# Turning operands with one vector instruction and sixteen on-chip transfers in a two-layer transformer trunk

## The chip, the cores and the metric

One NeuronCore of one Trainium2 chip runs the kernel. The metric is the device time of one execution in microseconds (us). TensorE is called PE here, VectorE DVE, ScalarE ACT, GpSimd POOL, and SP is the engine whose queue issues nearly all DMAs of this kernel.

## What is computed

Two layers of a transformer trunk on 256 tokens of width 2048, in float32. Cut to the lines that matter here:

```python
for i in range(2):
    if i == 0: h = h + even_mixer(h)   # sparse attention and gated linear attention
    else:      h = h + odd_mixer(h)    # q, k, v = split(rmsnorm(h) @ w_in); 16 heads, z = q @ k.T ...
    xn = rmsnorm(h, ffn_norm[i])
    h = h + (silu(xn @ w_gate) * (xn @ w_up)) @ w_down        # hidden width 5632
    gate = sigmoid(rmsnorm(h, ple_norm[i]) @ ple_w_gate[i])
    h = h + (p[i] @ ple_w_proj[i]) * gate
out = rmsnorm(h, final_norm)
```

PE sums over the partitions. So the left operand of each product, which has tokens along the partitions when it is made, has to be turned until its columns lie along the partitions.

## The kernel before, in words

**The stream of weights.** Every product with a weight matrix goes through `unit` (line 176): four chunks of 128 rows by 512 columns, 1 MB, come by one DMA on SP's queue (line 184) into a tile `raw`, of which there are two. For each half of it ACT casts a rounded part `whi` (line 99) and DVE subtracts it from `raw` for the rest `wlo` (line 100); there are four of each. PE then runs 12 products of 512 columns for a half, 24 for a unit (lines 201 to 203): left high part by `whi`, left high part by `wlo`, left low part by `whi`, for each chunk and each of the two halves of the tokens. A `block` (line 206) is the row of units, mostly four, that makes 512 output columns.

**Order of the work.** `later` (line 161) puts small pieces of work into a line, and `tick` (line 169) runs at most one of them after each half unit. A scheduler then orders the instructions of each engine, and each engine takes its own in that order. An instruction that waits holds up what stands behind it on its engine. That goes for SP too: a DMA whose source is not ready holds up the later ones. The program uses eight completion semaphores in turn for SP's DMAs, so a DMA also waits until the one eight places ahead has landed.

**Where operands are turned.** Three places, two ways:

- `h`, five times, for the norms after the first: `finish_cols` (line 224) takes each 512 columns of `h` when they are final, squares them on ACT, and queues two calls of `turn_h` (line 135). Each call turns two chunks of 128 columns by four PE transposes against an identity (line 141) into PSUM; ACT multiplies by the gain for the high part (line 146), DVE makes the low part (line 147). The first norm does the same while `x` arrives.
- the FFN's hidden block `sl` (line 802): four calls of `turn_blocks` (line 123), each four DVE transposes of 32 partitions by 256 columns (line 128) that write another quarter of the partitions; DVE turns blocks of 32 by 32. Then ACT and DVE split the result `hx` (lines 789, 790). There are 22 such blocks.
- q and k of the odd mixer, two tiles for each of four groups of heads, by `turn_blocks` as well, into `qT` and `kT`, which `scores` reads.

**Around them.** `mixer_out` (line 674) runs the first two output blocks in two parts, so that with 16 units its four column blocks end after units 6, 8, 12 and 16. The last `down` (line 809) of an FFN has two units a block, as 11 hidden blocks go in groups of 3, 3, 3 and 2. `gated` (line 861) is the sigmoid and two DVE operations on each half of the tokens. In the last stage `keep` (line 892) loads a quarter of the last columns' weights into a tile of its own, `kept`, four times.

Of the kernel before, what the change touches and what calls it, by code (L numbers as in the profile page):

```python
# [27 lines left out]
def trunk_kernel(ctx: ExitStack, tc: tile.TileContext, x, p, even_norm, even_w_in, even_w_gk,  # L28
# [36 lines left out]
    # the activation tables and the tensor engine's clock are up when the data comes  # L65
# [7 lines left out]
    # norm gains, one row of 128 per chunk, turned so that a chunk's gains lie along the partitions  # L73
# [61 lines left out]
    def turn_h(dst, norm, c2):  # L135
        """Chunks 2*c2 and 2*c2+1 of h, transposed, times the gain, split."""
# [39 lines left out]
    def unit(ps, stat, k0, cols, first, last, nk=KU, kw0=None, step=KU, pre=None):  # L176
        """nk chunks of the contraction: cols = [(weight, first column, width)]."""
# [28 lines left out]
    def block(stat, cols, nk=KC, key=None, ps=None, k0=0, k1=None, kw=0, pre=None):  # L206
        """Output columns over chunks k0..k1 of the contraction; returns the two PSUM tiles."""
# [43 lines left out]
    with tc.issue_after(got_gains.ins):  # L251
# [4 lines left out]
    # upb[s, c] = 1/16 where s <= c in one chunk of 64; sub[s, c] = 1/16 where s > c there  # L256
    upb = const.tile([P, P], F32, name="upb")
    nc.gpsimd.memset(upb, 0.0625)
    nc.gpsimd.affine_select(upb, upb, pattern=[[1, P]], compare_op=OP.is_ge, fill=0.0, base=0,
                            channel_multiplier=-1)  # L260
    nc.gpsimd.memset(upb[0:64, 64:128], 0.0)
    sub = stage("sub")[:, :P]
    nc.gpsimd.memset(sub, 0.0625)
    nc.gpsimd.affine_select(sub, sub, pattern=[[-1, P]], compare_op=OP.is_gt, fill=0.0, base=0,
                            channel_multiplier=1)
    nc.gpsimd.memset(sub[64:128, 0:64], 0.0)
    subr = const.tile([P, P], F32R, name="subr")
    nc.vector.tensor_copy(subr, sub)
    # keys no later than the query, in one chunk
    upm = upb.bitcast(I32)  # L270
    # strictly earlier keys, keys along the partitions
# [8 lines left out]
    # -1 where the first index is no earlier than the second  # L280
# [10 lines left out]
    def even_mixer(xs, ps0, ep):  # L291
# [3 lines left out]
        oT = new_act()  # L295

# [12 lines left out]
        def tokens(ps, name, w=NB):  # L309
            """The block's last w columns by tokens, scaled by the row's norm."""  # L310
# [7 lines left out]
        # u0: c (128), the last pair of q_idx (128), k_idx (64), zeros (64), k_idx again (64),  # L318
        # the gate's low-rank part (16), one
# [6 lines left out]
        # c and three pairs of q_idx  # L326
# [8 lines left out]
        # a pair of q_idx, k_idx, w_idx and the gate's low-rank part  # L335
# [71 lines left out]
        def index_heads(pairs, tt):  # L407
            """pairs: [(the pair's columns by tokens, its first head)]"""
# [574 lines left out]
```

## Time and profile before

| | |
|---|---|
| Median of 3 runs | 2440.72 us (2440.68 to 2441.49) |
| Profiled execution, first to last instruction (span) | 2438.5 us |
| Time beside the span (median less span) | 2.2 us |
| PE busy | 2417.6 us, 99% |
| DVE busy | 1506.6 us, 62% |
| ACT busy | 1154.1 us, 47% |
| DMA queue of SP | 447 MB, 55.6% of 16 engines' span |
| TensorE clock granted | nine tenths or more of full speed in all 40 slices |

The profile was taken of one execution, whose own time is known by its span alone; the median stands 2.2 us above it. Busy times are unions of instructions on an engine. Products overlap in PE's pipeline, so the mean duration of one is longer than the distance between two.

### The profile page before, as it was taken

To read this page: it belongs to the slowest core of one execution; us is meant where nothing else is said; L and a number is where in the kernel's file an instruction comes from. 1 tells how busy PE (TensorE), PEld (TensorE's weight loads), DVE (VectorE), ACT (ScalarE), POOL (GpSimd) and SP (SyncE) were. 2 spreads that over 40 slices of the span, in tenths; PEclk is the share of its full clock that TensorE was granted. 3 is DMA by queue.
4 is the path that set the end of the run, shared out by engine and by line. 5 is a ranking of instruction groups with operands and counts; after the bars stand their busy time and mean duration, and the time that the engine had idled before them with its cause. 6 is when DMAs were issued, how large, how long until landed. Compare 5 with 4: busy or idle time off the path is not lost.

```text
span 2438.5 us, 27647 instructions
## 1 busy us (share of the span) xinstructions
PE 2417.6 (99%) x10966; PEld 1996.5 (82%) x10966; DVE 1506.6 (62%) x1907; ACT 1154.1 (47%) x1418; POOL 19.2 (1%) x45
## 2 busy tenths in 40 slices
PE   8999999999999999999999999999999999999998
PEld 7887788888888888888888888888888888888887
DVE  5765555766756665655676666557667556556564
ACT  6644444344434434446546565544444344444463
POOL 0000000000000000000000000000000000000000
PEclk9999999999999999999999999999999999999999
DMA  6454455566556565555554454555655655556563
GB/s 211 147 169 151 144 194 186 189 196 201 189 192 193 186 205 183 198 190 185 178 190 156 161 184 165 180 190 177 203 190 192 205 190 186 196 187 206 182 231 123
DMA packets 231651, 450.01 MB, mean 185 GB/s; under 512 B 9457, under 2 KB 16337, under 8 KB 231394
## 3 DMA queue, kind: packets, MB, share of 16 engines
q1 hardware_dynamic: 231234, 447.07, 55.6%
q8 instruction: 86, 1.41, 0.2%
q10 hardware_dynamic: 288, 1.18, 0.1%
q14 instruction: 43, 0.35, 0.0%
HBM read 446.12 MB, written 2.10 MB: 184 GB/s over the span
## 4 chain that ended last, share of the span: by engine, by line
PE 91%; issue 5%; ACT 2%; DVE 1%; DMA 1%; SPq 0%; POOLq 0%; POOL 0%; DVEq 0%; ACTq 0%
PE mm L202 29%; PE mm L201 29%; PE mm L203 29%; PE at L141 1%; DVE kT L128 1%; DVE wlo L100 0%; DMA raw<-in_odd_w_in_dram 0%; PE at L424 0%; DMA h<-in_x_dram 0%; PE at L742 0%; DVE sp L719 0%; ACT whi L99 0%; ACT sp L716 0%; ACT sp L715 0%; ACT L715 0%
## 5 line engine op out<-in xcount | busy, mean ns | idle before, releaser
L100 DVE TENSOR_TENSOR wlo<-raw,whi 128x1024 fp32r<-128x1024 f32 (+2 forms) x848 | 1020.7, 1213 | 794.1 <-ACT whi L99 790.1
L99 ACT CAST whi<-raw 128x1024 fp32r<-128x1024 f32 (+2 forms) x848 | 874.8, 1042 | 1053.5 <-PE mm L203 668.8
L201 PE MATMUL mm<-whi,aH 128*128 128x512 f32 (+2 forms) x2656 | 1036.9, 390 | 0.7 <-ACT whi L99 0.7
L202 PE MATMUL mm<-wlo,aH 128*128 128x512 f32 (+2 forms) x2656 | 1028.8, 387 | 4.1 <-DVE wlo L100 4.1
L203 PE MATMUL mm<-whi,aL 128*128 128x512 f32 (+2 forms) x2656 | 1028.7, 387 | 0.0
L202 PEld LDWEIGHTS mm<-wlo,aH 128*128 128x128 f32 x2656 | 499.4, 188 | 104.7 <-DVE wlo L100 5.9
L203 PEld LDWEIGHTS mm<-whi,aL 128*128 128x128 f32 x2656 | 499.1, 188 | 103.4 <-issue 1.0
L201 PEld LDWEIGHTS mm<-whi,aH 128*128 128x128 f32 x2656 | 499.2, 188 | 102.9 <-issue 2.8
L201 PE MATMUL mm<-whi,hH 128*128 128x512 f32 x704 | 277.2, 394 | 0.0
L202 PE MATMUL mm<-wlo,hH 128*128 128x512 f32 x704 | 277.0, 393 | 0.0
L203 PE MATMUL mm<-whi,hL 128*128 128x512 f32 x704 | 273.6, 389 | 0.0
L128 DVE STREAM_TRANSPOSE hx<-sl 32x256 f32<-32x256 f32 x352 | 153.6, 436 | 6.1
L201 PEld LDWEIGHTS mm<-whi,hH 128*128 128x128 f32 x704 | 132.2, 188 | 30.0
L203 PEld LDWEIGHTS mm<-whi,hL 128*128 128x128 f32 x704 | 132.2, 188 | 29.7
L202 PEld LDWEIGHTS mm<-wlo,hH 128*128 128x128 f32 x704 | 132.4, 188 | 26.1
L146 ACT ACTIVATE aH<-at,gT 128x256 fp32r<-128x256 f32 x96 | 45.1, 473 | 51.4 <-DVE aL L147 47.5
L789 ACT CAST hH<-hx 128x1024 fp32r<-128x1024 f32 x22 | 23.2, 1054 | 92.6 <-DVE hx L128 92.6
L147 DVE SCALAR_TENSOR_TENSOR aL<-at,gT,aH 128x256 fp32r<-128x256 f32 x96 | 45.8, 480 | 22.0 <-ACT aH L146 21.9
L234 DVE TENSOR_TENSOR h<-mm,h 128x512 f32<-128x512 f32 x80 | 52.4, 682 | 2.7 <-PE mm L203 2.7
L141 PE MATMUL at<-ident,h 128*128 128x128 f32 x192 | 30.5, 283 | 5.0 <-DMA h<-in_x_dram 5.0
L141 PEld LDWEIGHTS at<-ident,h 128*128 128x128 f32 x192 | 24.9, 145 | 11.8 <-DMA h<-in_x_dram 3.0
L128 DVE STREAM_TRANSPOSE qT<-tok 32x256 f32<-32x256 f32 x64 | 27.9, 436 | 6.8 <-ACT tok L762 5.8
(221 smaller groups left out, 806.8 us busy)
## 6 DMA issues: line engine op xcount, KB each, us to landing
raw<-in_ffn_w_gate_dram SPq DMA_DIRECT2D x88, 1024.0 KB, 5.2
raw<-in_ffn_w_up_dram SPq DMA_DIRECT2D x88, 1024.0 KB, 5.2
raw<-in_ffn_w_down_dram SPq DMA_DIRECT2D x88, 1024.0 KB, 5.0
raw<-in_odd_w_in_dram SPq DMA_DIRECT2D x48, 1024.0 KB, 5.2
raw<-in_even_w_in_dram SPq DMA_DIRECT2D x36, 1024.0 KB, 5.0
raw<-in_ple_w_gate_dram SPq DMA_DIRECT2D x28, 1024.0 KB, 5.1
raw<-in_even_w_out_dram SPq DMA_DIRECT2D x16, 1024.0 KB, 5.1
raw<-in_odd_w_out_dram SPq DMA_DIRECT2D x16, 1024.0 KB, 5.0
```

What stands on the lines that cost most here:

```text
L99: nc.scalar.copy(hi, raw)
L100: nc.vector.tensor_tensor(lo, raw, hi.bitcast(F32), OP.subtract)
L128: nc.vector.transpose(dst[32 * a:32 * a + 32, :, :, 32 * q:32 * q + 32], src.rearrange("p t (m a c) -> p t m a c", a=4, c=32)[32 * q:32 * ...
L141: nc.tensor.transpose(ps[:, c, tt, :], h[:, tt, k * P:(k + 1) * P], ident)
L146: nc.scalar.activation(dst[0][:, k, :], src, AF.Copy, scale=g)
L147: nc.vector.scalar_tensor_tensor(dst[1][:, k, :], src, g, dst[0][:, k, :].bitcast(F32), op0=OP.mult, op1=OP.subtract)
L201: nc.tensor.matmul(ps[tt][:, :n], sh, hi[:, c, :n], start=st, stop=False)
L202: nc.tensor.matmul(ps[tt][:, :n], sh, lo[:, c, :n], start=False, stop=False)
L203: nc.tensor.matmul(ps[tt][:, :n], sl, hi[:, c, :n], start=False, stop=en)
L234: nc.vector.tensor_tensor(hs, ps[tt], hs, OP.add)
L789: nc.scalar.copy(d[0], t)
```

## The change

All operands after the first norm are turned in two steps. `cross` first runs one DVE transpose on all 128 partitions and 1024 columns: it turns each block of 32 by 32 where it lies, so that within each quarter of the partitions the columns come in the right place but tokens of four quarters stay apart. Then 16 DMAs on SP's queue, 32 KB each, carry 32 partitions of `tq` to 32 partitions of `tx`: each source quarter to each destination quarter. ACT and DVE read `tx` (views `crossed` and `flat` put it in order) and split it. `turn_blocks` goes, and `turn_h` remains for the first norm alone. The pool of `tq` (one buffer) and `tx` (two) is opened after the even mixer. To make room, the squares share the one buffer of the tag `stage`, two constants move into the even mixer's pool, the sigmoid's result stays in PSUM, and `keep` takes its place among the two `raw` tiles.

```diff
-    def turn_blocks(dst, src, a):
-        for q in range(4):
-            nc.vector.transpose(dst[32 * a:32 * a + 32, :, :, 32 * q:32 * q + 32],
-                                src.rearrange("p t (m a c) -> p t m a c", a=4, c=32)[32 * q:32 * q + 32, :, :, a, :])
+    pools = {}
+    def cross(src):
+        tq = pools["x"].tile([P, 4, NT, 4, 32], F32, name="tq", bufs=1)
+        nc.vector.transpose(tq.rearrange("p a t m r -> p t m a r"),
+                            src.rearrange("p t (m a c) -> p t m a c", a=4, c=32))
+        x = pools["x"].tile([P, 8, 4, 32], F32, name="tx")
+        for a in range(4):
+            for q in range(4):
+                nc.sync.dma_start(x[32 * a:32 * a + 32, q::4], tq[32 * q:32 * q + 32, a])
+        return x
+    def crossed(x):
+        return x.rearrange("p q m r -> p m q r")
+    def flat(t):
+        return t.rearrange("p m (q r) -> p m q r", q=8)
...
+    def gain_h(dst, norm, x, c2):
+        for k in (2 * c2, 2 * c2 + 1):
+            g = gT[1][:, (norm - 1) * KC + k:(norm - 1) * KC + k + 1]
+            src = crossed(x)[:, k % 4]
+            hi, lo = (flat(d[:, k:k + 1, :])[:, 0] for d in dst)
+            nc.scalar.activation(hi, src, AF.Copy, scale=g)
+            nc.vector.scalar_tensor_tensor(lo, src, g, hi.bitcast(F32), op0=OP.mult, op1=OP.subtract)
...
     def finish_cols(nx, cb):
         for tt in range(NT):
             square_sum(nx["key"], tt, cb, h[:, tt, cb * NB:(cb + 1) * NB])
+        x = {}
+        first = (nx["key"], "x", cb)
+        later(lambda: x.update(x=cross(h[:, :, cb * NB:(cb + 1) * NB])), key=first)
         for c2 in (2 * cb, 2 * cb + 1):
-            later(lambda c2=c2: turn_h(nx["dst"], nx["norm"], c2), key=(nx["key"], c2))
+            later(lambda c2=c2: gain_h(nx["dst"], nx["norm"], x["x"], c2), key=(nx["key"], c2), after=(first, 2))
...
-                for a in range(4):
-                    later(lambda t=t, d=dst, a=a: turn_blocks(d.rearrange("p t (m c) -> p t m c", c=P), t, a))
+                x = {}
+                later(lambda t=t, x=x: x.update(x=cross(t)), key=("x3", g, i))
+                later(lambda d=dst, x=x: nc.scalar.copy(flat(d), crossed(x["x"])), after=(("x3", g, i), 2))
...
-                hx = fp.tile([P, 4, NT * P], F32, name="hx")
-                for a in range(4):
-                    later(lambda d=hx, t=sl, a=a: turn_blocks(d.rearrange("p m (t c) -> p t m c", t=NT), t, a))
-                later(lambda t=hx, n=n, gi=gi: split_hid(hT[gi], t, 4 * n), key=("hT", i, b))
+                x = {}
+                later(lambda t=sl, x=x: x.update(x=cross(t)), key=("xT", i, b))
+                later(lambda x=x, n=n, gi=gi: split_hid(hT[gi], x["x"], 4 * n), key=("hT", i, b),
+                      after=(("xT", i, b), 2))
...
-            raw = pp.tile([P, KU, HB], F32, name="kept", bufs=1)
+            raw = wp.tile([P, KU, NB], F32, name="raw", bufs=2)[:, :, :HB]
```

**What the order of the instructions becomes.** Three places. In the names, `raw` is a unit's 1 MB of weights, `tq` the tile after the DVE transpose, `tx` the tile after the transfers; the numbers tell buffers of the same name apart.

SP at an FFN block's end, before: the four loads of the next block's weights.

```order
L184 DMA raw_3435<-in_ffn_w_gate_dram 128x4x512
L184 DMA raw_3473<-in_ffn_w_gate_dram 128x4x512
L184 DMA raw_3515<-in_ffn_w_gate_dram 128x4x512
L184 DMA raw_3555<-in_ffn_w_gate_dram 128x4x512
L184 DMA raw_3594<-in_ffn_w_up_dram 128x4x512
```

Now:

```order
L208 DMA raw_3473<-in_ffn_w_gate_dram 128x4x512
L208 DMA raw_3526<-in_ffn_w_gate_dram 128x4x512
L208 DMA raw_3562<-in_ffn_w_gate_dram 128x4x512
L135 DMA tx_3509<-tq_3507 32x2x128 x16
L208 DMA raw_3596<-in_ffn_w_gate_dram 128x4x512
```

The sixteen transfers stand between the third and the fourth load. All 22 FFN blocks and the eight tiles of q and k have this pattern.

SP in the last `down` of the first FFN (its eight units are raw_7794 to raw_8130), now; before, the same loads stood in a row:

```order
L208 DMA raw_7924<-in_ffn_w_down_dram 128x4x512
L208 DMA raw_7970<-in_ffn_w_down_dram 128x4x512
L135 DMA tx_7907<-tq_7905 32x2x128 x16
L208 DMA raw_8027<-in_ffn_w_down_dram 128x4x512
L135 DMA tx_8010<-tq_8008 32x2x128 x16
L208 DMA raw_8073<-in_ffn_w_down_dram 128x4x512
L135 DMA tx_8113<-tq_8111 32x2x128 x16
L208 DMA raw_8130<-in_ffn_w_down_dram 128x4x512
```

Three times sixteen transfers stand among the last three loads, one load between two of them.

DVE at the same place, now: mm_7968 and mm_7969 are the sums of the third column block.

```order
L261 TENSOR_TENSOR h_73<-mm_7968,h_73 128x512
L261 TENSOR_TENSOR h_73<-mm_7969,h_73 128x512
L130 STREAM_TRANSPOSE tq_8111<-h_73 128x8x4x32
L172 SCALAR_TENSOR_TENSOR aL_7791<-tx_8010,gT5_95,aH_7790 128x256 x4
L100 TENSOR_TENSOR wlo_8076<-raw_8073,whi_8075 128x1024
L100 TENSOR_TENSOR wlo_8096<-raw_8073,whi_8095 128x1024
```

The subtraction for the seventh unit (raw_8073) stands behind the sums of the third block, which end when that seventh unit should begin on PE; before, the same subtractions (raw_7998 is the seventh unit there, mm_7902 and mm_7903 are the sums) stood ahead of them, with one for the eighth (raw_8041):

```order
L100 TENSOR_TENSOR wlo_8001<-raw_7998,whi_8000 128x1024
L100 TENSOR_TENSOR wlo_8017<-raw_7998,whi_8016 128x1024
L147 SCALAR_TENSOR_TENSOR aL_7730<-at_7938,gT5_95,aH_7729 128x256 x2
L100 TENSOR_TENSOR wlo_8044<-raw_8041,whi_8043 128x1024
L147 SCALAR_TENSOR_TENSOR aL_7730<-at_7965,gT5_95,aH_7729 128x256
L234 TENSOR_TENSOR h_73<-mm_7902,h_73 128x512
L147 SCALAR_TENSOR_TENSOR aL_7730<-at_7965,gT5_95,aH_7729 128x256
```

The work that waits for PE's last product of the block has moved ahead of the subtractions that PE's next unit needs.

## Rows read from the trace of the kernel before

**Rows 1.** The page, part 1: busy time of each engine.

```profile
PE 2417.6 (99%) x10966; PEld 1996.5 (82%) x10966; DVE 1506.6 (62%) x1907; ACT 1154.1 (47%) x1418; POOL 19.2 (1%) x45
```

**Rows 2.** Waits of PE: who waited for whom, us in total, times, longest.

```profile
PE mm L202 <- DVE wlo L100: 4.1, 5, 0.8
PE mm L201 <- ACT whi L99: 0.7, 2, 0.5
```

**Rows 3.** Timeline of PE round one turn of `h`: start us, us, what.

```profile
1200.20 0.39 PE L202 MATMUL mm<-wlo,aH 128*128 128x512 f32 x1
1200.43 0.39 PE L203 MATMUL mm<-whi,aL 128*128 128x512 f32 x1
1200.66 0.60 PE L141 MATMUL at<-ident,h 128*128 128x128 f32 x4
1201.02 0.48 PE L201 MATMUL mm<-whi,aH 128*128 128x512 f32 x1
1201.33 0.40 PE L202 MATMUL mm<-wlo,aH 128*128 128x512 f32 x1
```

**Rows 4.** Groups by line and shape: count, busy us, mean ns, idle before.

```profile
L141 PE MATMUL at<-ident,h 128*128 128x128 f32 x192 | 30.5, 283 | 5.0 <-DMA h<-in_x_dram 5.0
L128 DVE STREAM_TRANSPOSE hx<-sl 32x256 f32<-32x256 f32 x352 | 153.6, 436 | 6.1
L147 DVE SCALAR_TENSOR_TENSOR aL<-at,gT,aH 128x256 fp32r<-128x256 f32 x96 | 45.8, 480 | 22.0 <-ACT aH L146 21.9
L100 DVE TENSOR_TENSOR wlo<-raw,whi 128x1024 fp32r<-128x1024 f32 x832 | 1010.4, 1223 | 779.8 <-ACT whi L99 775.9
L99 ACT CAST whi<-raw 128x1024 fp32r<-128x1024 f32 x832 | 865.5, 1050 | 1040.2 <-PE mm L203 661.2 <-DMA raw<-in_ffn_w_up_dram 152.9 <-DMA raw<-in_odd_w_in_dram 68.9
```

**Rows 5.** Timeline of SP: three small transfers issued in a row.

```profile
17.39 0.33 SPq L80 DMA_DIRECT2D graw<-in_ffn_norm_dram  x1
17.77 0.42 SPq L80 DMA_DIRECT2D graw<-in_ple_norm_dram  x1
18.23 0.42 SPq L80 DMA_DIRECT2D graw<-in_odd_norm_dram  x1
```

**Rows 6.** DMA issues: count, KB each, median us to landing; then line L80's landings.

```profile
raw<-in_ffn_w_gate_dram SPq DMA_DIRECT2D x88, 1024.0 KB, 5.2
kept<-in_ple_w_gate_dram SPq DMA_DIRECT2D x4, 512.0 KB, 6.0
...
DMA to landing us min/median/max: 1.6/2.8/4.2
```

**Rows 7.** Timelines of SP, ACT and DVE round one end of an up block.

```profile
757.38 0.37 SPq L184 DMA_DIRECT2D raw<-in_ffn_w_gate_dram  x1
766.29 0.37 SPq L184 DMA_DIRECT2D raw<-in_ffn_w_gate_dram  x1
...
760.48 1.05 ACT L99 CAST whi<-raw 128x1024 fp32r<-128x1024 f32 x1 [1.67 <-PE mm L203]
763.20 1.06 ACT L99 CAST whi<-raw 128x1024 fp32r<-128x1024 f32 x1 [1.67 <-PE mm L203]
...
759.99 1.40 DVE L802 SCALAR_TENSOR_TENSOR sl<-mm,rstd,sl 128x512 f32<-128x512 f32 x2
761.43 3.57 DVE L128 STREAM_TRANSPOSE hx<-sl 32x256 f32<-32x256 f32 x8
765.03 1.23 DVE L100 TENSOR_TENSOR wlo<-raw,whi 128x1024 fp32r<-128x1024 f32 x1
```

**Rows 8.** Timelines of ACT and DVE at a gated block's end.

```profile
1147.45 1.27 ACT L864 ACTIVATE sgm<-mm,rstd 128x512 f32<-128x512 f32 x2
...
1149.38 1.28 DVE L867 TENSOR_TENSOR h<-h,sgm 128x512 f32<-128x512 f32 x2
```

**Rows 9.** Windows after the last product: busy times, granted clock, DMA share, GB/s.

```profile
2431.00:2434.00 3.00, 0.00 (x0) 0.00 (x0) 1.59 (x5) 1.15 (x3) 0.56 (x1) 1.00 0.19 72
2434.20:2438.40 4.20, 0.00 (x0) 0.00 (x0) 0.00 (x0) 0.00 (x0) 0.00 (x0) 0.50 0.54 181
```

More of the change, by code (lines that the diff above doesn't have):

```diff
@@ L107, in square_sum @@
             ss[key] = sm.tile([P, NT, 4], F32, name="ss")
-        scr = sm.tile([P, NB], F32, name="sqs", bufs=1)
+        scr = sm.tile([P, NB], F32, name="sqs", tag="stage", bufs=1)
         nc.scalar.activation(scr, src, AF.Square, accum_out=ss[key][:, tt, cb:cb + 1])
@@ L253, in trunk_kernel @@
     done.update((("n0", i), 0) for i in range(KC // 2))
[L257 to L270, printed above, removed]
     diag = const.tile([P, P], F32, name="diag")
@@ L295, in even_mixer @@
         oT = new_act()
+        upb = ep.tile([P, P], F32, name="upb", bufs=1)
+        nc.gpsimd.memset(upb, 0.0625)
+        nc.gpsimd.affine_select(upb, upb, pattern=[[1, P]], compare_op=OP.is_ge, fill=0.0, base=0,
+                                channel_multiplier=-1)
+        nc.gpsimd.memset(upb[0:64, 64:128], 0.0)
+        sub = stage("sub")[:, :P]
+        nc.gpsimd.memset(sub, 0.0625)
+        nc.gpsimd.affine_select(sub, sub, pattern=[[-1, P]], compare_op=OP.is_gt, fill=0.0, base=0,
+                                channel_multiplier=1)
+        nc.gpsimd.memset(sub[64:128, 0:64], 0.0)
+        subr = ep.tile([P, P], F32R, name="subr", bufs=1)
+        nc.vector.tensor_copy(subr, sub)
+        upm = upb.bitcast(I32)
         def t2(name, dt=F32):
@@ L623, in outputs @@
             for a in range(2):
-                scr = sm.tile([P, NB], F32, name="sqs", bufs=1)
+                scr = sm.tile([P, NB], F32, name="sqs", tag="stage", bufs=1)
                 nc.scalar.activation(scr[:, :256], ov[g][:, tt, a * 256:(a + 1) * 256], AF.Square,
@@ L672, in even_mixer, with mixer_out_first, mixer_out @@
         return oT
-    def mixer_out(oT, W, nx):
+    def mixer_out_first(oT, W):
         for i in range(4):
             need(("oT", i))
-        part = {}
-        for cb in range(2):
-            part[cb] = block(oT, [(W, cb * NB, NB)], k1=8)
+        part = [block(oT, [(W, cb * NB, NB)], k1=8) for cb in range(2)]
         for i in range(4, 8):
             need(("oT", i))
+        return part
+    def mixer_out(oT, W, nx, part):
         for cb in range(4):
-            ps = block(oT, [(W, cb * NB, NB)], ps=part.get(cb), k0=8 if cb < 2 else 0)
+            ps = block(oT, [(W, cb * NB, NB)], ps=part[cb] if cb < 2 else None, k0=8 if cb < 2 else 0)
             add_to_h(ps, cb)
@@ L708, in scores @@
                 pz = at_tile()
[L709 removed]
+                nc.tensor.matmul(pz[:, 0:256], kT[:, j, 0:P], qT[:, j, :], start=True, stop=False,
                                  skip_group_check=True)
[L711 removed]
+                nc.tensor.matmul(pz[:, 256:384], kT[:, j, P:], qT[:, j, P:], start=False, stop=False,
                                  skip_group_check=True)
@@ L758, in odd_mixer @@
                     nc.vector.tensor_scalar(rq, rs, float(128 ** -0.5), None, op0=OP.mult)
-                dst = op.tile([P, NT, NB], F32, name="qT" if i == 0 else "kT")
+                dst = op.tile([P, 4, NT * P], F32, name="qT" if i == 0 else "kT")
                 t = op.tile([P, NT, NB], F32, name="tok")
@@ L785, in ffn, with split_hid @@
         hT = {}
-        def split_hid(dst, t, k0):
-            d = [dst[n][:, k0:k0 + 4, :] for n in range(2)]
-            nc.scalar.copy(d[0], t)
-            nc.vector.tensor_tensor(d[1], t, d[0].bitcast(F32), OP.subtract)
+        def split_hid(dst, x, k0):
+            hi, lo = (flat(dst[n][:, k0:k0 + 4, :]) for n in range(2))
+            nc.scalar.copy(hi, crossed(x))
+            nc.vector.tensor_tensor(lo, crossed(x), hi.bitcast(F32), OP.subtract)
         def gate_up(gi):
@@ L861, in gated @@
         def gated(pg, tt, c0, w):
-            sgm = pp.tile([P, NB], F32, name="sgm", bufs=2)[:, :w]
-            nc.scalar.activation(sgm, pg[:, :w], AF.Sigmoid, scale=rs[:, tt:tt + 1])
-            nc.vector.tensor_tensor(sgm, sgm, eb[c0 // NB][tt][:, c0 % NB:c0 % NB + w], OP.mult)
+            nc.scalar.activation(pg[:, :w], pg[:, :w], AF.Sigmoid, scale=rs[:, tt:tt + 1])
+            e = eb[c0 // NB][tt][:, c0 % NB:c0 % NB + w]
+            nc.vector.tensor_tensor(e, pg[:, :w], e, OP.mult)
             hs = h[:, tt, c0:c0 + w]
-            nc.vector.tensor_tensor(hs, hs, sgm, OP.add)
+            nc.vector.tensor_tensor(hs, hs, e, OP.add)
         if not last:
@@ L885, in squared @@
             c0, w = parts[n]
-            scr = sm.tile([P, NB], F32, name="sqs", bufs=1)
+            scr = sm.tile([P, NB], F32, name="sqs", tag="stage", bufs=1)
             nc.scalar.activation(scr[:, :w], h[:, tt, c0:c0 + w], AF.Square, scale=float(D ** -0.5),
@@ L939, in trunk_kernel @@
         nx = start_norm("n1", 1)
-        mixer_out(oT, even_w_out[0], nx)
+        part = mixer_out_first(oT, even_w_out[0])
+    pools["x"] = ctx.enter_context(tc.tile_pool(name="xp", bufs=2))
+    mixer_out(oT, even_w_out[0], nx, part)
     with tc.tile_pool(name="fp0", bufs=2) as fp:
@@ L950, in trunk_kernel @@
         nx = start_norm("n4", 4)
-        mixer_out(oT, odd_w_out[0], nx)
+        mixer_out(oT, odd_w_out[0], nx, mixer_out_first(oT, odd_w_out[0]))
     with tc.tile_pool(name="fp1", bufs=2) as fp:
```

2 lines of the change are left out of this document (removed).

## The prediction

> **What bounds the kernel now.** I read the page's busy times first: PE is busy 99% of the span [rows 1]. Then PE's waits: in the whole run it stood 4.1 and 0.7 us for split weights, never over 0.8 us at once [rows 2]. So PE sets the time; whatever takes work off it gains at once, and whatever makes weights late costs at once. Third, the timelines round a block's end, for how much cover the weights have.
>
> PE starts a product every 0.227 us: 2.72 us between the two casts that wait for it, divided by 12 [rows 7]. A unit of 24 lasts 5.45 us. Let S be the time when PE ends a block and starts unit u0 of the next; in [rows 7] it is 760.48, where the second cast for u1 is released by PE. The load of u2 was issued at 757.38, S - 3.1, while PE needs u2 at S + 10.9: a lead of 14.0 us. It needs 5.2 us to land [rows 6], then a cast and a subtraction, 1.05 and 1.22 us [rows 4], with some 0.2 us between them; the subtraction is wanted 0.23 us after the unit's first product. So a unit may be issued up to **7.4 us** before its start (5.2 + 2.5 - 0.3) without a stall, and it has **6.6 us** to spare. The load of u3, normally at S + 2.35, was issued at 766.29, S + 5.8, since the DVE transposes held up the subtractions; PE did not stall, which agrees.
>
> **What the change removes.** 160 of the 192 PE turns of `h` go (32 belong to the first norm) [rows 4]: 40 groups of four. In [rows 3] the products at 1200.43 and 1201.33 are two products apart beside one group: 0.90 us where 0.45 is normal. So a group costs 0.45 to 0.46 us, and 40 cost **18.4 us**, all on the bounding engine. DVE loses 480 transposes of 0.436 us, 209 us (352 for hidden blocks [rows 4], 128 alike for q and k). Nothing of that is gained: PE hardly waited for DVE.
>
> **What it adds.** 50 crossings (20 for `h`, 22 for hidden blocks, 8 for q and k). Each is one DVE transpose and 16 transfers.
>
> The transpose, 128 by 1024, is not in the trace. 32 by 256 takes 0.436 us, and other operations of 256 columns on all 128 partitions 0.480, of 1024 columns 1.22 [rows 4]: time follows columns, not partitions. I take **1.23 us**; four passes would be 4.9 us, the upper bound. DVE's new total, 62 us, lies beside PE's work, as do the eight copies of q and k on ACT (1.05 us each, 8 us).
>
> The 16 transfers wait at the head of SP's queue for the transpose, and the next loads wait behind them. Three small transfers in a row start 0.38 and 0.46 us apart [rows 5]. I take 0.46, since there the one ahead followed another directly: **7.4 us** a crossing. Low end 0.38: 6.1 us. High end: each transfer waits for the one eight places ahead to land; small ones landed in 1.6 to 4.2 us [rows 6], so 4.2 / 8 = 0.53 us, 8.4 us a crossing. Below 3.7 us of landing that wait costs nothing.
>
> **Where loads come late**, by the order of the instructions; stall = time of issue less the deadline of 7.4 us before the unit's start:
>
> - Hidden block (22 times): the two products on DVE end at 761.39 [rows 7], S + 0.9; transpose to S + 2.15; transfers to S + 9.55. Then u3, due by S + 16.35 - 7.4 = S + 8.95: 0.6 us each, 13.2.
> - q and k (8): transpose to S + 1.95, 0.4 us each, 3.2.
> - `mixer_out` (twice): the first crossing as above, 0.6. The second comes two units later with one load between: the transfers end 9.55 after the block, only then is the load of two units on issued, and it lands at 14.75; subtracted at 17.1, wanted at 11.7: 5.4. The third has four loads ahead: nothing. The fourth has a subtraction ahead of its transpose, 2.0. Together 8.0, twice: 16.0.
> - Last `down` (twice), two units a block: 0.6 and 5.4 as before. The third crossing starts at S + 2.15 of the unstalled third block, 13.65 after the second block's end; transfers to 21.05; the last load lands at 26.25, subtracted at 28.6, wanted at 22.6 after the stall before: 6.0. The fourth has two subtractions ahead of its transpose: it ends at S + 4.4, 2.9. Together 14.9, twice: 29.8.
> - `ple` of the first layer: sigmoids to the final `h` take 3.2 us (1147.45 to 1150.66 [rows 8]), of which 0.7 lies ahead of S; with a subtraction and the transpose S + 5.3, transfers to 12.7, 3.75 late. Three such, 11.25 (the first has four loads ahead). At the second block DVE's order puts a product and an addition of that block ahead of the subtraction for the next unit, which PE then awaits 2.5 us. Together 13.75.
> - `keep` now takes a `raw` tile four times: one tile remains for the stream, and its cycle is 5.2 + 3.5 = 8.7 us against 5.45. Four units lose up to 5.45 + 3 x 3.2 = 15, of which 6.6 are covered: 0 to 8.4, I take 4. Its transfer took 6.0 us beside others [rows 6].
>
> Sum of losses: 13.2 + 3.2 + 16.0 + 29.8 + 13.75 + 4 = 80 us. Less 18.4: **+61.6 us**, a span of 2438.5 + 61.6 = 2500.1, and with the 2.2 us beside the span, **2502 us** against the median of 2440.7. The rest I cost at nothing: squares sharing `stage` wait for an earlier user that is done long before (uncovered, one landing of 5.2 us, once); the gain's operations on ACT and DVE keep number and shape; the sigmoid in PSUM holds its bank 1.3 us longer, with two blocks of banks there.
>
> **Rivals.** *A, on the other side: issues are cheap.* The place is SP behind the transpose. If a transfer cost under 0.09 us there, 16 would end by S + 3.6, and no load would be late, save where DVE's order alone holds PE. That is at the seventh unit of each last `down` (sum 0.7 after S, transpose 1.23, four gains 1.9, subtraction 1.22: 4.8 us, twice) and at the 2.5 us in `ple`, 12 in all, and with the 4 of `keep` 16. The time is 2440.7 - 18.4 + 16 = 2438, or 2422 if these are covered too. It decides from 7.4 us down to 1.5. For it: no row shows an on-chip transfer. Against: small transfers took SP 0.33 to 0.42 us each [rows 5], a load of 1 MB 0.37 [rows 7]. The Trainium skill, DMA: Bandwidth & Descriptors, section Anatomy of one DMA — SWDGE (gpsimd) path, puts the sequencer's dispatch of a DMA at about 50 ns; by that sixteen would take an estimated 0.8 us and this rival would hold. That section is on another issuing path, and the rows above differ from it.
>
> *B: transfers land slowly.* At 4.2 us each the wait for the one eight places ahead decides, 8.4 us a crossing. 47 crossings (all but the three with four loads ahead) lose 1.0 us more: 2502 + 47 = 2549. For it: one small transfer did take 4.2 us to land [rows 6]. Against: at most blocks no load is in flight when the crossing starts.
>
> *C: the transpose does not run on all partitions at once.* 4.9 us instead of 1.23 puts 47 crossings 3.7 later: 2502 + 174 = 2676. Against it: the rows above. A smaller addition that may ride on any: a stalled PE may get the lower clock. It was granted 1.00 in 2431 to 2434 with nothing running, 0.50 after [rows 9]. Six stalls are over 5 us; if each ran a unit at 1.2 in place of 2.4 GHz, that is 6 x 5.45 = 33 us.
>
> **How the numbers follow.** Chances: forecast 0.72, A 0.13 (half of it at 2422, half at 2438), B 0.12, C 0.03. Within the forecast, 0.38 us an issue brings the 30 hidden blocks and tiles to nothing (-16.4) and 17 others 1.2 us down (-20): 2466; without `keep`'s 4, 2462. The top is B with most of the clock's 33: 2575. So the range is 2462 to 2575; it leaves out A, C and little more. A measurement of this kernel can tell about 0.2%, 4.9 us. Faster by more comes from A's better half, 0.07; the other half is within 0.2%, 0.06; slower 0.87.
>
> **What would show it.** SP issues of `tx` 0.46 us apart; loads behind them late; in PE's waits `whi` and `wlo` with some 80 us instead of 5, the longest 5 to 6 us in the last `down` of either FFN and in `mixer_out`; a hidden block's end with a stall under 1 us; one DVE transpose of about 1.23 us; no PE turns past the first norm. I am wrong if the issues are under 0.2 us apart, if PE's waits stay under 20 us, or if waits of 3 us and more stand at every hidden block, which would say that the slack of 6.6 us is not there.

## The result and the profile after

The changed kernel takes **2747.5 us** (median of 4 runs, 2737.7 to 2756.2) against 2441.1 us: a ratio of 1.125 (95% interval 1.1225 to 1.1282). I forecast 2502 us, at most 2575. The sign was right, the loss five times too small: +306 us for +62. The profiled execution has a span of 2740.6 us, 302 more than that of before.

Busy times (PEld is PE's loading of the turned operand) and the shares of the chain that ended last (SPq is SP's queue), from the page of after; [rows 1] has the busy times of before:

```profile
PE 2524.4 (92%) x10806; PEld 2038.0 (74%) x10806; DVE 1351.9 (49%) x1477; ACT 1164.2 (42%) x1426; POOL 19.2 (1%) x45
...
PE 55%; SPq 16%; DMA 13%; DVE 8%; ACT 6%; issue 3%; ACTq 0%; DVEq 0%; POOLq 0%; POOL 0%
```

Two things happened to PE. It stood 216 us (2740.6 - 2524.4) where it stood 21. And it was busy 107 us longer with 160 instructions fewer. The second is the clock, below. SP's queue, 0% of the chain before, holds 16% of it.

PE's waits, in us in total, times, longest; [rows 2] answer to the first two:

```profile
PE mm L225 <- ACT whi L99: 172.9, 54, 6.1
PE mm L226 <- DVE wlo L100: 18.4, 29, 1.4
PE at L738 <- ACT kT L794: 5.7, 4, 2.2
```

What PE waits for is the cast and the subtraction of the weights, as forecast, 191 us instead of the 80. What the transfers cost, from the answer for their line (durations in ns: least, median, greatest), and the transpose, from that for the tile `tq`:

```profile
L135 SPq DMA_DIRECT2D tx<-tq x800: 585/595/1749, 334.5 to 2625.8; - x160
...
DMA to landing us min/median/max: 1.8/1.9/6.5
```

```profile
L130 DVE STREAM_TRANSPOSE tq<-sl x22: 1245/1246/1247, 455.4 to 2475.4; 128x1024 f32<-128x1024 f32 x22
```

The transpose is 1.25 us (forecast 1.23). The transfers land in 1.9 us. But one holds SP for 0.595 us, and they start 0.64 apart, not 0.46: 16 of them take 10.2 us and not 7.4 in 27 of the 50 crossings, and up to 12.45 us in the others, where single ones took longer. One of the 27, from SP's timeline:

```profile
506.82 10.18 SPq L135 DMA_DIRECT2D tx<-tq  x16
```

The next hidden block's end, one of the longer ones, from the timeline of after (start, duration; in brackets the idle time before and what ended it):

```profile
555.29 11.05 SPq L135 DMA_DIRECT2D tx<-tq  x16
566.44 0.53 SPq L208 DMA_DIRECT2D raw<-in_ffn_w_gate_dram  x1
...
568.96 0.39 PE L227 MATMUL mm<-whi,aL 128*128 128x512 f32 x1
...
571.99 1.99 ACT L99 CAST whi<-raw 128x1024 fp32r<-128x1024 f32 x2 [3.01 <-DMA raw<-in_ffn_w_gate_dram]
...
573.08 1.22 PE L225 MATMUL mm<-whi,aH 128*128 128x512 f32 x2 [3.73 <-ACT whi L99]
```

Sixteen transfers, then the load; 5.5 us after its issue it has landed and the cast starts; PE stood 3.7 us. Each link is the one I forecast. The same place in windows (length, busy time of each engine with its instructions, then PE's granted clock, share and rate of the DMAs):

```profile
core 0: us, PE busy (x) PEld busy (x) DVE busy (x) ACT busy (x) POOL busy (x), PEclk, DMA share, GB/s
562.00:569.00 7.00, 7.00 (x33) 5.76 (x31) 0.00 (x0) 1.05 (x1) 0.00 (x0) 1.00 0.30 68
569.00:572.50 3.50, 0.35 (x2) 0.00 (x0) 1.23 (x1) 0.52 (x1) 0.00 (x0) 0.89 1.04 400
572.50:576.00 3.50, 2.88 (x6) 1.87 (x7) 2.63 (x3) 2.83 (x4) 0.00 (x0) 0.50 0.39 142
576.00:579.00 3.00, 3.00 (x9) 2.34 (x9) 2.09 (x2) 0.65 (x1) 0.00 (x0) 0.57 0.76 207
579.00:583.00 4.00, 4.00 (x19) 3.30 (x18) 0.00 (x0) 2.04 (x3) 0.00 (x0) 1.00 0.97 360
...
424.00:1143.60 719.60, 682.13 (x2870) 552.71 (x2870) 345.82 (x308) 276.72 (x276) 0.00 (x0) 0.96 0.56 185
```

After PE stood, the clock was granted at 0.50 of full, 1.2 in place of 2.4 GHz, for some 7 us: 9 products in 3 us where there are 19 in 4 us afterwards. The last row is the stretch with the first FFN's 11 hidden crossings; before, it took 660.60 us, all busy:

```profile
397.60:1058.20 660.60, 660.60 (x2910) 545.61 (x2909) 411.70 (x476) 275.84 (x279) 0.00 (x0) 1.00 0.59 193
```

So this stretch grew by 59.0 us: 37.5 us of standing (3.4 us a block) and 21.5 us more of busy time for the same products (2.0 a block).

The whole difference by stage. A stage is bounded by the same two of the 848 casts of weights in each kernel's trace; where a stage's last crossings act on the first units of the next, the bound is three units on. Each figure is the stretch less that of before, in us; "half speed" is the time after at a granted clock of 0.50 (nearly 5 us of the last `ple`'s lie behind the last product, where before has 4). A cast that bounds a stage can itself be late (the one at the start of the first FFN's stretch comes 13.3 us behind the one ahead in after, 3.2 in before), so a few us can lie on the other side of a bound; the negative figures of the hidden blocks need not be gains.

| Stretch | forecast, PE turns deducted | after | of it at half speed | POOL issues (E2) | five transfers (E6) | all on DVE (E8) | two stages (E12) |
|---|---|---|---|---|---|---|---|
| even mixer | 0 | +0.7 | 0 | 0.0 | +0.2 | +0.1 | +1.8 |
| `mixer_out`, both | +8.6 | +47.5 | 31 | +10.9 | +4.4 | +4.6 | -6.1 |
| hidden blocks, 22 | +13.2 | +120.4 | 115 | +2.7 | -5.6 | -4.2 | 0.0 |
| last `down`, both | +22.4 | +55.9 | 35 | +22.8 | +19.2 | +8.3 | +0.1 |
| first `ple` | +10.1 | +25.0 | 21 | +9.4 | +3.8 | +5.1 | -0.1 |
| odd mixer (q and k) | +3.2 | +39.4 | 34 | +18.8 | +9.1 | -1.3 | -0.4 |
| last `ple` (`keep`) | +4.0 | +13.1 | 15 | +11.6 | +15.4 | +11.1 | 0.0 |
| sum | +61.5 | +302.0 | 251 | +76.2 | +46.5 | +23.7 | -4.7 |

### The profile page after: what moved, and what is told of

It is laid out like the page before. It is cut to its first block, busy times and chain, and to the rows that moved or that the text cites. A ratio compares the mean times of both kernels' runs of the same rounds, so it can differ in the third digit from the quotient of the medians.

```text
span 2740.6 us, 28088 instructions
## 1 busy us (share of the span) xinstructions
PE 2524.4 (92%) x10806; PEld 2038.0 (74%) x10806; DVE 1351.9 (49%) x1477; ACT 1164.2 (42%) x1426; POOL 19.2 (1%) x45
## 4 chain that ended last, share of the span: by engine, by line
PE 55%; SPq 16%; DMA 13%; DVE 8%; ACT 6%; issue 3%; ACTq 0%; DVEq 0%; POOLq 0%; POOL 0%
PE mm L226 18%; PE mm L227 17%; PE mm L225 17%; SPq L135 16%; DMA raw<-in_ffn_w_gate_dram 4%; DVE wlo L100 4%; ACT whi L99 3%; DMA raw<-in_ple_w_gate_dram 2%; DVE tq L130 2%; DMA raw<-in_odd_w_in_dram 2%; DMA raw<-in_ffn_w_down_dram 2%; DVE sl L832 1%; DMA raw<-in_ffn_w_up_dram 1%; DMA raw<-in_odd_w_out_dram 0%; DVE h L261 0%
## 5 line engine op out<-in xcount | busy, mean ns | idle before, releaser
L225 PE MATMUL mm<-whi,aH 128*128 128x512 f32 (+2 forms) x2656 | 1060.3, 402 | 129.3 <-ACT whi L99 129.3
L226 PE MATMUL mm<-wlo,aH 128*128 128x512 f32 (+2 forms) x2656 | 1064.2, 401 | 16.1 <-DVE wlo L100 15.3
L227 PE MATMUL mm<-whi,aL 128*128 128x512 f32 (+2 forms) x2656 | 1055.4, 397 | 0.0
L226 PEld LDWEIGHTS mm<-wlo,hH 128*128 128x128 f32 x704 | 137.5, 195 | 40.3 <-DVE wlo L100 10.2
L820 DVE TENSOR_TENSOR hL<-tx,hH 128x1024 fp32r<-128x1024 f32 x22 | 27.0, 1226 | 169.0 <-ACT hH L819 169.0
L819 ACT CAST hH<-tx 128x1024 fp32r<-128x1024 f32 x22 | 23.1, 1051 | 172.8 <-DMA tx<-tq 172.8
L171 ACT ACTIVATE aH<-tx,gT 128x256 fp32r<-128x256 f32 x80 | 34.3, 497 | 100.8 <-DMA tx<-tq 100.8
L172 DVE SCALAR_TENSOR_TENSOR aL<-tx,gT,aH 128x256 fp32r<-128x256 f32 x80 | 33.3, 479 | 83.1 <-ACT aH L171 83.1
L829 ACT ACTIVATE sl<-mm,rstd 128x512 f32<-128x512 f32 x44 | 29.9, 688 | 72.0 <-PE mm L227 72.0
L109 ACT ACTIVATE sqs<-h 128x512 f32<-128x512 f32 x48 | 30.3, 631 | 33.5 <-DVE h L261 33.0
L832 DVE SCALAR_TENSOR_TENSOR sl<-mm,rstd,sl 128x512 f32<-128x512 f32 x44 | 30.9, 744 | 0.0
```

The source lines that it names most:

```text
L171: nc.scalar.activation(hi, src, AF.Copy, scale=g)
L172: nc.vector.scalar_tensor_tensor(lo, src, g, hi.bitcast(F32), op0=OP.mult, op1=OP.subtract)
L225: nc.tensor.matmul(ps[tt][:, :n], sh, hi[:, c, :n], start=st, stop=False)
L226: nc.tensor.matmul(ps[tt][:, :n], sh, lo[:, c, :n], start=False, stop=False)
L227: nc.tensor.matmul(ps[tt][:, :n], sl, hi[:, c, :n], start=False, stop=en)
L832: nc.vector.scalar_tensor_tensor(sl[:, tt], pu[tt], rs[:, tt:tt + 1], sl[:, tt], op0=OP.mult, op1=OP.mult)
```

## The experiments

**The theory** after the result: the mechanism is the one forecast, loads held up on SP, but an on-chip transfer is dearer to issue than any row of before showed, and each wait that this makes brings a stretch of half clock, which I had priced for six waits only. **Rivals:** PE waits for the turned operands or for DVE; the transfers crowd the loads on the DMA engines; the side edits (`keep`, the sigmoid in PSUM) cost much of it; the clock costs nothing of its own.

**E1, the price alone.** Groups of transfers with nothing beside them, in this order: as in the change; 32 rows with 1 KB in one piece; 128 rows; 8 rows; 32 rows from DRAM; 1 MB of weights; as in the change on ACT's queue and on POOL.

```diff
+    for fn in (as_is, whole, tall, few_rows, from_dram, weights, on_act, on_pool):
+        go(fn)
```

> Leaves out the whole computation: eight groups of transfers alone, 16 of each kind (8 for the last weights), one group after the other. Theory (the on-chip transfer itself is dearer to issue than the small loads I took the price from): groups of 32 rows on chip are issued on SP 0.60 to 0.66 us apart with nothing else running, the 32-row loads from DRAM 0.33 to 0.46, the 1 MB weight loads about 0.37. Rival 1 (the price is that of a busy queue, lanes still in flight from weights): alone they come 0.46 us apart or less. Rival 2 (the price is per row or per piece): 8 rows under 0.3 us, 128 rows over 1 us, one piece of 1 KB a row instead of two of 512 B cheaper by a fifth or more.

The timeline of SP, ACT and POOL (start, time from the first issue's start to the last one's end). The first group is left out, as a store of 2 MB fell into it; the lines are the second to fifth group, then ACT's and POOL's:

```profile
21.39 10.07 SPq L68 DMA_DIRECT2D s<-s  x16
31.57 10.18 SPq L72 DMA_DIRECT2D s<-s  x16
41.86 11.20 SPq L76 DMA_DIRECT2D s<-s  x16
53.19 7.62 SPq L80 DMA_DIRECT2D s<-in_even_w_in_dram  x16
...
102.57 10.36 ACTq L89 DMA_DIRECT2D s<-s  x16
...
115.66 8.57 POOL L93 DMA_DIRECT2D s<-s  x16 [6.38 <-DVE s L47]
```

From SBUF to SBUF: 0.63 us apart for 32 rows in one piece, 0.64 for 128 rows, mostly 0.67 for 8 (median duration 0.624). From DRAM: 0.46, the price I had read off small loads. So neither rows, bytes nor pieces set it. ACT pays the same, POOL 0.53. Both rivals fall. That the source lies in SBUF is not what costs either: transfers out of SBUF into DRAM are as cheap as loads, those of before's output and those of E6 below (durations in ns as above):

```profile
L934 SPq DMA_DIRECT2D out_dram<-h x8: 333/398/445, 2427.0 to 2434.0; - x8
L135 SPq DMA_DIRECT2D td<-tq x200: 303/432/2427, 334.0 to 2360.7; - x100
```

So it is the transfer with both ends on chip that is dearer, by some 0.18 us. One store does not fit: the 2 MB here held SP for 0.586 us. The Trainium skill, DMA: Bandwidth & Descriptors, section Anatomy of one DMA — SWDGE (gpsimd) path, says of GpSimd's path that many descriptors can go out before the incremental cost shows; on SP's queue the rows go the same way, 8 to 128 rows at nearly one price. Its 50 ns for the dispatch, which spoke for my rival A, is no price for a whole issue: 0.536 us was measured on POOL and 0.6 us on SP.

**E2, the same transfers issued by POOL.**

```diff
-                nc.sync.dma_start(x[32 * a:32 * a + 32, q::4], tq[32 * q:32 * q + 32, a])
+                nc.gpsimd.dma_start(x[32 * a:32 * a + 32, q::4], tq[32 * q:32 * q + 32, a])
```

> Same transfers, same bytes, issued by POOL instead of SP. Theory (the loads of weights come late because they stand behind 16 issues on SP; everything else follows from that): PE's idle time falls from 216 us to under 50, the clock stays at 1.00 outside the first norm, and the time is 2422 to 2455 us. Rival 1 (PE waits for the turned operands or for DVE, whoever issues): over 2700 us still. Rival 2 (the transfers crowd the weights' transfers on the DMA engines): the loads land later than 5.2 us and the time stays over 2600 us.

2515.3 us, ratio 1.030 (1.0284 to 1.0315), clock 0.987. The stretch of the hidden blocks, then PE's waits:

```profile
401.40:1061.30 659.90, 657.06 (x2889) 541.77 (x2888) 348.43 (x312) 278.15 (x279) 96.93 (x183) 1.00 0.63 202
```

```profile
PE at L738 <- ACT kT L794: 17.5, 4, 7.1
PE mm L225 <- ACT pe L886: 15.3, 2, 11.1
PE mm L226 <- DVE wlo L100: 14.3, 17, 1.5
PE mm L225 <- ACT whi L99: 12.7, 8, 2.6
PE mm L225 <- ACT aH L171: 11.4, 3, 6.9
```

Three quarters of the loss (232 of 306 us) goes with the queue, with the same bytes on the same DMA engines, so the loads are held on SP and not by crowding. Hidden blocks lose next to nothing now (+2.7). I missed the 2455: PE still stood 88 us (span 2514.6, busy 2426.5), where I expected under 50, and the clock still fell. Of its waits 29 us are for the operand itself (`kT`, `aH`), which SP's had covered, 27 for split weights and 15 for `pe`, the first tiles of the last stage (E9). 16 transfers at 0.53 us still take 8.6 us, and where a stage needs them at once (`kT`, `aH`) PE stands up to 7 us. So the first rival holds a small part. The Trainium skill, Perfetto Trace Analysis, section DMA Optimizations, says that spreading DMAs over the engines that can issue them may help when generating their descriptors is the bottleneck; this run agrees, by 232 us.

**E3, four transfers to a half unit, on SP.**

```diff
+        for a in range(4):
+            later(lambda a=a: send(a), key=key if a == 3 else None)
```

> All 16 transfers stay on SP, but four go out per half unit, so that weight loads get in between. Theory (0.64 us an issue against a slack of 6.6 us): four issues are 2.6 us, within the slack, so the 22 hidden blocks and the 8 of q and k stop stalling (about 30 x 3.1 us of waiting and 30 x 1.9 us of half-speed products, 150 us in all); the ends of mixer_out, the last down and ple keep part of theirs, since the fills of one column block now number six and run into the next. 2480 us (2440 to 2560). Rival (the total of SP's issue time, not its being in one piece, holds the loads): over 2680 us.

2702.0 us, ratio 1.107 (1.105 to 1.1087): it seems to bear out the rival. But SP's timeline shows that the edit took effect in part only. At a hidden block, and in the last `down` of the first FFN:

```profile
501.06 10.19 SPq L134 DMA_DIRECT2D tx<-tq  x16
...
1171.76 6.66 SPq L134 DMA_DIRECT2D tx<-tq  x8
1178.52 0.54 SPq L210 DMA_DIRECT2D raw<-in_ffn_w_down_dram  x1
1179.10 5.62 SPq L134 DMA_DIRECT2D tx<-tq  x8
```

At the hidden blocks and at q and k all 16 still stand in one piece, so the time of the run says nothing about either side. By stages it goes with the theory: where the piece stayed whole nothing was gained (hidden blocks +122.9, odd mixer +44.3), and where it came apart the two last `down` fell from +55.9 to +18.6 together and the two `mixer_out` from +47.5 to +36.2. Other work moved there too, so this is a sign and no test; E5 is the test.

**E5, the same for the hidden blocks alone, tied to the order of the loads.**

```diff
+        def behind(a):
+            with tc.issue_after(state["load"].ins):
+                send(a)
...
+                later(lambda a=a: behind(a) if a else send(a), key=key if a == 3 else None, delay=(2, 7, 9, 11)[a])
```

> The 22 hidden blocks' transfers alone are spread on SP, and this time tied to the order of the loads: four behind the transpose as before, and each further four behind the next unit's load. Bytes, count and queue stay. Theory (0.64 us an issue, 10.2 us in one piece, against a slack of 6.6 us): pieces of 2.6 us fit, so a hidden block takes 43.5 us as it did with POOL issuing, in place of 49.6: 2747 - 22 x 6.1 = 2613 us (2595 to 2650). Rival (the total of SP's time, not the piece, holds the loads): hidden blocks stay at 49 us, over 2720 us.

2619.1 us, ratio 1.072 (1.0702 to 1.0738); expected 2613. SP's timeline and the stretch of the hidden blocks:

```profile
498.23 2.51 SPq L134 DMA_DIRECT2D tx<-tq  x4
500.84 0.53 SPq L218 DMA_DIRECT2D raw<-in_ffn_w_gate_dram  x1
501.41 2.50 SPq L134 DMA_DIRECT2D tx<-tq  x4
504.01 0.55 SPq L218 DMA_DIRECT2D raw<-in_ffn_w_up_dram  x1
```

```profile
421.60:1077.20 655.60, 654.48 (x2869) 539.86 (x2870) 347.39 (x308) 275.23 (x275) 0.00 (x0) 1.00 0.63 203
```

Bytes, number and queue of the transfers stayed, only their places in the order changed, and the hidden blocks' 120 us are gone, to within 6 us of the forecast of this run. SP's total time for them is about the same, so what costs is the length of one piece against the slack: 2.6 us fit, 10.2 do not.

**E6, five transfers through DRAM in place of 16 on chip.** `tq` and `tx` lie by quarters here, and the low part of `h` is made by two instructions a chunk.

```diff
+        td = pools["d"].tile([P, 4, 256], F32, name="td")
+        for q in range(4):
+            nc.sync.dma_start(td.rearrange("(a r) q n -> q r a n", a=4)[q], tq[32 * q:32 * q + 32])
+        nc.sync.dma_start(x, td)
```

> Each crossing goes through DRAM in five transfers in place of 16: four of 32 rows out, one of 128 rows back. Theory (SP's time goes by the number of transfers, not by bytes): 4 x 0.64 + 0.46 = 3.0 us of issuing and some 2 us in which the last waits for the four to land, so SP is through by S + 7.3, inside the 8.95 at which u3's load is due: hidden blocks at 43.5 us, q and k likewise; the ends of mixer_out, down and ple keep a third of theirs. 2480 us (2440 to 2540). Rival (twice the bytes, and DRAM, cost more than the issues saved): over 2650 us.

2487.6 us, ratio 1.019 (1.0173 to 1.0203), 260 us less than after; expected 2480. SP's timeline at two hidden blocks, and what the fifth transfer waited for on SP (us in total, times, longest):

```profile
520.22 3.32 SPq L135 DMA_DIRECT2D td<-tq  x4
523.63 0.40 SPq L211 DMA_DIRECT2D raw<-in_ffn_w_gate_dram  x1
526.11 0.34 SPq L136 DMA_DIRECT2D tx<-td  x1
...
563.73 1.78 SPq L135 DMA_DIRECT2D td<-tq  x4
```

```profile
SPq L136 <- DMA td<-tq: 98.5, 92, 3.7
```

The data moves twice, and yet it is the fastest of the versions with transfers: what counts is how long one piece holds SP, not the bytes. Here that is shorter twice over, by fewer issues and by a lower price of one: the four out of SBUF into DRAM mostly took 1.78 us together, not the 2.6 that I expected. SP did wait for their landing, 2.0 us a crossing, as expected, but one load mostly went ahead of that wait.

**E4 and E7, the clock.** Products that nobody reads, put where PE stands: 12 at each of the 30 ends of hidden blocks, q and k (E4); 18 at the 22 hidden blocks alone (E7).

```diff
+            if state["unit"] in busy:
+                sp = at_tile()
+                for _ in range(18):
+                    nc.tensor.matmul(sp, stat[0][:, k0, 0:P], stat[0][:, k0:k0 + 2, :], start=True, stop=True)
```

> The kernel after, with 360 products added that nobody reads: 12 ahead of the half unit that waits in each of the 30 blocks of hidden and q/k (12 x 0.227 = 2.7 us where PE stands 2.6 to 3.9 us). Theory (a third of the loss is the clock at half speed after each wait, about 1.9 us a stall): with the wait filled the clock stays at 1.00 there, and more work takes less time: 2747 - 30 x 1.9 = 2690 us (2670 to 2710). Rival (the clock falls for another reason than PE's standing idle): 2747 us or more, with the clock still 0.50 after these places.

> The kernel after, with 396 products that nobody reads: 18 (4.1 us) ahead of the half unit that waits, in the 22 hidden blocks only; in the run with 12, PE still stood 0.8 and 1.3 us at each of these places and the clock still fell after every second one. Theory (the clock goes to half because PE stood, and half-speed products are the rest of what a hidden block loses): the clock stays at 1.00 through both feed-forwards, a hidden block takes 43.5 + 4.1 + 0.2 = 47.8 us in place of 49.6, and 2747 - 22 x 1.8 = 2707 us (2695 to 2725). Rival (the clock costs nothing that the waits would not have cost anyway): 2747 us or more, hidden blocks at 49.6 us or more.

E4: 2751.6 us, ratio 1.127 (1.1251 to 1.1286), no change to after: a miss. E7: 2728.8 us, ratio 1.118 (1.1159 to 1.1194), 19 us less than after with 396 products more. The stretch of the first FFN's hidden blocks, in E4 and in E7:

```profile
424.90:1141.50 716.60, 695.38 (x2994) 567.19 (x2995) 345.45 (x308) 274.19 (x276) 0.00 (x0) 0.99 0.56 185
```

```profile
423.70:1131.00 707.30, 700.96 (x3060) 574.93 (x3061) 345.13 (x308) 273.89 (x275) 0.00 (x0) 1.00 0.57 188
```

In E7 PE stood 6.3 us in this stretch, not 37.5, and the clock stayed at full speed. That is the test of the clock's price: after's busy 682.1 and 198 products at 0.227 us (44.9) would be 727.0; measured 701.0. Against before, the same products took 21.5 us longer in after. So the half clock cost some 22 to 26 us of busy time in this FFN, 2.0 to 2.4 us a block, and it follows from PE's standing. The gain in time is smaller (12.3 and 9.8 us in the two FFNs), since the added products take up the time in which PE stood. In E4 12 products were too few (21 us of standing left in this stretch, the clock falling at every second block), and at q and k they stood in places where PE did not wait: the odd mixer grew by 17.5 us, which ate the gain of the FFNs, 3.0 and 10.9 us.

**E9, the side edits in `ple` undone in the kernel after.** The room comes from closing the pool of `tq` and `tx` ahead of the last `ple`.

```diff
-            nc.scalar.activation(pg[:, :w], pg[:, :w], AF.Sigmoid, scale=rs[:, tt:tt + 1])
+            sgm = pp.tile([P, NB], F32, name="sgm", bufs=2)[:, :w]
+            nc.scalar.activation(sgm, pg[:, :w], AF.Sigmoid, scale=rs[:, tt:tt + 1])
...
-            raw = wp.tile([P, KU, NB], F32, name="raw", bufs=2)[:, :, :HB]
+            raw = pp.tile([P, KU, HB], F32, name="kept", bufs=1)
```

> The kernel after with the two edits in ple undone: the sigmoid has its sgm tiles again and keep its own kept tile (room comes from closing the crossing's pool ahead of the last ple). Theory (the crossing makes nearly all of the loss, these two edits only that of the last ple): the last ple, 13.1 us longer than before in the run of after, falls to under 4, the first ple, 25 us longer, by 3 or less; 2747 - 12 = 2735 us (2725 to 2742). Rival (the sigmoid in the PSUM bank holds back the next block): the first ple falls by 8 us or more, under 2725 us.

2749.0 us, ratio 1.126 (1.1242 to 1.1273): as after. By stretches, the last `ple` fell from +13.1 to +3.6 as expected, and the first stayed at +25.1, so the sigmoid in PSUM does not hold back the next block. But the last `down` ahead of it rose from +26.0 to +35.1, by one new wait:

```profile
PE mm L226 <- ACT pe L887: 18.2, 2, 15.3
```

The copies into `pe`, the first tiles of the last stage, come late; that they wait for the closed pool's memory is likely (in E11, where the last crossing ends two blocks sooner, this wait is gone) but was not taken apart. So the two edits cost some 9.5 us, and undoing them in this way gives as much back.

**E8, E10, E11, E12: without transfers.** E8 turns everything, `h` too, by the 16 quadrant instructions of before; E10 is E8 with the side edits undone as in E9 and the squares in a tile of their own; E11 is E10 with the last two column blocks of `h` turned on PE; E12 is E11 with DVE taking the first two blocks in `mixer_out` alone.

```diff
+        for q in range(4):
+            nc.vector.transpose(dst[32 * a:32 * a + 32, q::4],
+                                src.rearrange("p t (m a c) -> p t m a c", a=4, c=32)[32 * q:32 * q + 32, :, :, a, :])
...
+        if cb >= 2 or nx["norm"] not in (1, 4):
+            for c2 in (2 * cb, 2 * cb + 1):
+                later(lambda c2=c2: turn_h(nx["dst"], nx["norm"], c2), key=(nx["key"], c2))
+            return
```

> No transfer and no turn on PE: everything, h too, goes by 16 quadrant instructions on DVE, four to a half unit. Theory (PE bounds, DVE's 0.436 us instructions are hidden while loads come on time): the 18.4 us of PE's turns are gained and part is given back where DVE's queue delays the subtractions at the ends of mixer_out, down and ple: 2430 us (2420 to 2450). Rival (h's operand comes late at the start of every stage, since 16 instructions of 0.436 us take four half units, 11 us): 2450 to 2500 us.

2466.4 us, ratio 1.010 (1.0088 to 1.0118): the rival's range. PE's waits here are above all `wlo` (13.7 us in 17 waits, none over 1.5) and DVE's additions to `h` (6.9), then `whi` (4.9): DVE's queue at the ends of the stages, not the operand.

> The version with 16 quadrant instructions on DVE for everything, with sgm, kept and the squares' tile as in the kernel before. There the two ple cost 5.1 and 11.1 us against before, though no transfer is in it. Theory (that is the borrowed raw tile and the sigmoid in PSUM): 2466 - 13 = 2453 us (2446 to 2459). Rival (DVE's queue at the ends of ple): 2464 us or more.

2473.4 us, ratio 1.013 (1.0116 to 1.0147): slower than E8, a miss. The last `ple` fell from +11.1 to +3.9, and the last `down` rose from +4.9 to +17.0 by one wait for `pe` of 16.3 us, as in E9.

> As the run before it, but the last two column blocks of h in each stage are turned on PE again, by turn_h: only the first two, whose operand is not wanted soon, go by DVE. PE keeps 20 groups of 0.46 us and loses 20, 9 us. Theory (what is lost at the ends of the stages comes from the last column blocks, late behind DVE's queue): 2441 - 9 + 5 = 2437 us (2430 to 2445). Rival (it is DVE's total load): 2450 us or more.

2442.9 us, ratio 1.0006 (0.9997 to 1.0015): the same as before. With the last two blocks on PE, 30 of E10's 32 us are gone (16 of them the wait for `pe`), while DVE's busy time fell only from 1638.8 to 1572.7 us, against 1506.6 in before: it was mainly the late blocks that cost, not DVE's total. But the gain in the two `mixer_out` (-5.4 us) is given back in the last `down` (+3.9) and the first `ple` (+5.6).

> As the mix, but the first two column blocks go by DVE in the two mixer_out alone (8 groups of four PE turns fewer, 8 x 0.46 = 3.7 us); everywhere else h is turned on PE as before. In the mix the two mixer_out took 1.9 and 3.5 us less than before, the last down and the first ple 2.1, 1.8 and 5.6 more. Theory (a stage gains its turns where DVE's queue has room, and loses more where it has not): 2441 - 5 = 2436 us (2434 to 2439), faster than both kernels by some 0.2%. Rival (the gains of a stage are given back at the next, as PE ahead of its time meets loads that set the pace): 2440 to 2443 us.

**2435.8 us, ratio 0.998 (0.9969 to 0.9987)**: 5.7 us less than before, 0.2%, and the runs of the two do not overlap (2435.1 to 2437.4 against 2440.1 to 2442.9). Its `mixer_out` stretches take 6.1 us less than before, and every other is within 0.4 but the even mixer (+1.8). PE has 32 turns fewer and is busy 3.3 us less. The line of busy times:

```profile
PE 2414.3 (99%) x10934; PEld 1994.2 (82%) x10934; DVE 1532.7 (63%) x1971; ACT 1157.7 (48%) x1426; POOL 19.2 (1%) x45
```

## Why the prediction was right and wrong

- **Where it would be lost: right.** Loads behind the transfers on SP come late, and PE waits for their cast (172.9 us in 54 waits); without the transfers ahead of the loads (E2), or with short pieces (E5), that is gone where it was tried. The slack was right too: with 10.2 us for the transfers my rule gives 0.6 + 2.8 = 3.4 us a hidden block, and 3.4 us of standing was measured. To the tenth that is luck: the waits at the blocks ran from 2.4 to 4.0 us, and the pieces took 10.2 to 11.1 us in that stretch.
- **The step that failed first: "I take 0.46, since there the one ahead followed another directly", 7.4 us a crossing, at most 8.4.** It measured 0.64 us and 10.2 us. The price came from loads out of DRAM, which do cost 0.46 (E1); a transfer from SBUF to SBUF costs 0.18 more, and no row of before showed one. The high end was no bound: it allowed for a wait on the landing, but took the issue itself as known. 47 crossings x 2.8 us = 132 us, which makes the 80 of stalls 212; PE stood 195 us more than before. Because the slack was nearly used up at 7.4 us, 39% more on the price made the stall of a hidden block almost six times as long.
- **The step that failed second: "Six stalls are over 5 us", 33 us for the clock, as an addition that "may ride on any".** It came after waits of 2 to 4 us as well: of 47 waits over 2 us past the first norm, 45 were followed by a granted clock of 0.50. PE's busy time rose by 107 us while 18.4 us of turns left it: some 125 us, which is a difference and not a measurement of the clock. Another estimate: PE was busy for 208 of the 251 us at half speed, and half of that is 104. So the clock made some 100 to 125 us of busy time, a third or more of the whole loss; what that is in time is less sure, as slow products also overlap waits that would have come anyway. E7 shows its price in one FFN (22 to 26 us) and its cause.
- **The removed work: right in size (0.46 us a group), nothing of it seen** in after. E12 realises it where nothing is late: 3.7 us expected, 3.3 less of busy time measured; its two `mixer_out` took 6.1 less and the even mixer ahead of them 1.8 more.
- **The transpose** at 1.23 us: 1.25; rival C falls. **Landing** at 1.9 us, so rival B falls as well: the transfers were slow at the front, not at the end. **Rival A** fell on the price, yet in E2 the loads are on time at the hidden blocks, as it described, and 74 us are still lost: A left out the wait for the operand itself.
- **`keep`** at 4 us (0 to 8.4): with the sigmoid's edit about 9.5 (E9), a little over the high end, and 7.2 where nothing is transferred (E8 to E10).
- **What I said would refute me came near enough:** waits over 3 us at 13 of the 22 hidden blocks, of 2.4 us and more at all. I took that sign to say "that the slack of 6.6 us is not there"; the slack was there, and the piece on SP was longer.

## What to carry to other kernels

The price of a DMA on its issuing queue is a price per transfer, and it depends on what the transfer joins, here most on whether both ends lie on chip: take it from a row of the same kind or, where there is none, do not let the nearest kind be a bound. Where a cover is nearly used up, a small error in a price shows in full at every repetition, so price how far the sum is from the cover's edge, and give the repetitions a range that crosses it. Here nearly every wait of PE over 2 us had a second part, a stretch at half clock; a change that makes many such waits is priced with it at each.

## What the runs showed of the hardware that was not expected

- A transfer from SBUF to SBUF holds SP 0.595 us and ACT 0.607 whether it moves 32 rows or 128 (0.599); one of 32 rows from DRAM 0.42, one from SBUF into DRAM 0.43 (E6), a load of 1 MB 0.37. On POOL the first kind took 0.536.
- Adding 396 products shortened the run by 19 us, as PE then kept its full clock at nearly all hidden blocks.
- Waits of the same length did not always bring the lower clock: waits of 2.5 and 2.2 us past the first norm were not followed by it, others of 1.7 us were. What decides was not tried.
